# Two-layer encoder trunk on one core: where exponentials, reciprocals, a norm's operands, key copies and the first parameters are issued

## The chip, the core and the metric

One NeuronCore of a Trainium2 chip. The metric is the device time of one execution in microseconds (us). The engines of the core run side by side, each taking its own queue of instructions in order: TensorE (PE in the profile, with its weight loads as PEld), VectorE (DVE), ScalarE (ACT), GpSimd (POOL) and SyncE (SP), which here issues DMA transfers. They meet at semaphores.

## The reference, cut to what matters

The input is 512 tokens of width 1024, with 256 memory tokens. Each of two layers adds three terms to `x`:

```python
for l in range(DEPTH):
    x = x + hybrid_mixer(rms_norm(x, norm_mix[l]), w_in[l], na_rpb[l], q_norm[l], k_norm[l], w_out[l], ...)
    x = x + memory_cross_attention(rms_norm(x, norm_mem_q[l]), rms_norm(mem, norm_mem_kv[l]), w_q, w_kv, w_o)
    x = x + conv_ffn(rms_norm(x, norm_ffn[l]), w_up[l], conv_w[l], conv_b[l], w_down[l])
return rms_norm(x, norm_final)
```

The mixer projects `h` once to six parts. Eight heads do a 2-D neighbourhood attention (NA) with a learned bias, `softmax(q k / 8 + bias) v` over a window of the 8 x 64 grid. Eight query heads over two key heads do full attention (GQA); there q and k are normalised per head and rotated (rope) first. Both results go through `w_out`. The memory attention has 4 heads over 256 tokens; the feed-forward part is a SwiGLU with a depthwise convolution of width 3. Everything is float32.

## The kernel before

**Precision.** A float32 product is made of three matmuls. Each operand is split into `hi` (rounded to the type fp32r) and `lo = value - hi`, and `mm3` (L374) issues hi·hi, hi·lo and lo·hi into one PSUM bank. Weights are split by `emit_split`: `hi` by ACT (L290), `lo` mostly by POOL (L291).

**Layout.** `x` lies transposed in eight tiles `xT[c]` of 128 features x 512 tokens. A projection is 8 features' chunks x 3 matmuls = 24 matmuls of 128x512. PSUM has eight banks: four with tag `mm`, two `sc` (scores), two `tr` (transposes and small sums).

**Order.** PE's instructions keep the order in which the program writes them (`Counted`), as do those of engines named `..._IN_ORDER`. The instructions of ACT, DVE and POOL are put in order by a list scheduler that simulates the engines and picks by priority; `behind(n)` gives the instructions in its block a priority n places later (earlier for a negative n), and `tc.issue_after(i)` forces those of the same engine behind instruction `i`. Buffers from a pool (`tmp()`: 14 slots of 128x512; `ps_mm()`: 4 banks) are taken when the scheduler comes to the first instruction that writes them.

**Start (L386 to L405, L613 to L638).** `FIRST` lists the loads of the first three weights, cut in pieces, and of the eight `xT`. All are issued by SP, but the first weight piece and, behind it, the eight gains of the first norm, `par[:, 0, 0:8]` (L404), by ACT. `Norm.operand` (L464) makes `hi = x·gain` on ACT and `lo = x·gain - hi` on DVE.

**NA stage.** `weave` (L170) runs the four units' steps: in step s, `na_transpose(s-2)`, a piece of filler, `na_normalise(s-1)`, `na_scores(s)`, filler, `na_values(s-2)`, filler. A filler piece is some 2.5 us of matmuls from the projections (`project_qk`, `project_v`, `gqa_project`). `na_scores` (L778) writes two `sc` banks, DVE adds the bias and takes minima (L797), ACT takes four exponentials with their sums (L803). `na_normalise` (L807) takes the reciprocal of the sums on DVE (L809) and scales on POOL (L522) and ACT (L815). `na_values` (L834) multiplies by v into `mm` banks; ACT copies half of each (L849), DVE adds (L850, L851).

**Projections.** `split_qk` evicts q and k: ACT writes hi (`split_q` L738, `split_k` L720 and L722), DVE lo (L740, L724, L726). K is wanted in both halves of the partitions. For the very first k (`near`) ACT and DVE write both halves; for all others SP doubles it by DMA. `project_v` evicts with L518 (ACT) and L519 (DVE). `gqa_rope` (L895) reads its bank three times: two DVE products L901 and L902, then ACT's squares L903; a later piece, `split` (L933), multiplies the rotated value by its norm (L934). `reads` collects ACT's readings of PSUM banks in program order.

**Memory norm.** `memory_prepare` (L555) makes hi and lo of the 8 chunks of the memory (128x256 each): hi on ACT (L567), lo on DVE (L568), two chunks a step while the NA stage ends.

Of the kernel before, what the change touches and what calls it, by code (L numbers as in the profile page):

```python
# [18 lines left out]
P = 128  # L19
# [164 lines left out]
def encoder_kernel(ctx: ExitStack, tc: tile.TileContext, t: dict, out: bass.AP):  # L184
# [198 lines left out]
            mm3(ps, wh[:, k, c], wl[:, k, c], *ops[k], k == first, k == last)  # L383


    xT = [xpool.tile([P, S], F32, tag=f"x{c}", name=f"xT{c}") for c in range(KC)]  # L386
    par = cpool.tile([P, DEPTH, NPAR], F32, name="par")
    ones = cpool.tile([P, 1], F32, name="ones")
    nc.vector.memset(ones, 1.0)
# [3 lines left out]
    first_loads = []  # L393
    for n in FIRST:
        if isinstance(n, int):
            SP.dma_start(xT[n], t["xT"][n * P : (n + 1) * P, :])
            continue
        u, k0, k1 = n
        if u == len(first_loads):
            first_loads.append(raw_tile())  # L400
        raw, loads = first_loads[u]
        (nc.scalar if n == FIRST[1] else SP).dma_start(raw[:, k0:k1], loads[0][1][:, k0:k1])
        if n == FIRST[1]:
            nc.scalar.dma_start(par[:, 0, 0:8], t["par"][:, 0, 0:8])  # L404
    ACT_IN_ORDER.copy(small(1), ones)  # L405
    qkg = cpool.tile([P, DEPTH, 2], F32, name="qkg")
    gfin = cpool.tile([P, KC], F32, name="gfin")
# [37 lines left out]
    class Norm:  # L445


        def __init__(self, gcol=None, l=None, cols=slice(0, S)):
            self.gcol, self.l, self.acc, self.last, self.cols, self.n = gcol, l, None, None, cols, cols.stop - cols.start
            if gcol is not None:  # L450
                self.hi, self.lo = [xpool.tile([P, KC, S], F32R, tag="xg", name=nm("xg"), bufs=2) for _ in range(2)]
                self.ops = [(self.hi[:, c, :], self.lo[:, c, :]) for c in range(KC)]

        def close(self, c, pm):


            DVE.tensor_add(pm, pm, xT[c])
            DVE.tensor_copy(xT[c], pm)
            closed.append(self.operand(c, src=pm, rank=-25).ins)
            self.square(c)  # L460
            if c == KC - 1:
                closed.clear()

        def operand(self, c, act=ACT, src=None, dve=DVE, hi_only=False, lo_only=False, rank=0):  # L464
            src = xT[c] if src is None else src
            g = par[:, self.l, self.gcol + c : self.gcol + c + 1]
            hi, lo = self.ops[c]
            e = None if lo_only else act.activation(hi, src, AF.Copy, scale=g)
            if not hi_only:
                with behind(rank):  # L470
                    dve.scalar_tensor_tensor(lo, src, g, f(hi), op0=ALU.mult, op1=ALU.subtract)
            return e
# [82 lines left out]
    def memory_prepare(l):  # L555

        mops.clear()
        raw = load_mem()
        yield
        for c in range(KC):  # L560
            if c % 2 == 0:
                mg = rtile((2, 2, MEMN))
            g = par[:, l, G_MKV + c : G_MKV + c + 1]
            hi, lo = mg[:, 0, c % 2, :], mg[:, 1, c % 2, :]
            src = raw[c // 4][:, c % 4, :]
            with behind(40):
                ACT.activation(hi, src, AF.Copy, scale=g)  # L567
                DVE.scalar_tensor_tensor(lo, src, g, f(hi), op0=ALU.mult, op1=ALU.subtract)  # L568
            mops.append((hi, lo))
            if c % 2 == 1:  # L570
                yield

    mem_rstd = cpool.tile([P, MB], F32, name="mem_rstd")
# [38 lines left out]

    warm_up(N_WARM)  # L613
    nn = Norm(G_MIX, 0)
    DVE_IN_ORDER = InOrder(tc, nc.vector)
    for n in FIRST:
        if isinstance(n, int):
# [25 lines left out]
    for l in range(DEPTH):  # L643
# [73 lines left out]
        def split_k(pm, kt, near):  # L717
            rows = [(slice(64 * j, 64 * j + 64), slice(64 - 64 * j, 128 - 64 * j)) for j in range(2)]
            for k, (r, o) in zip(kt, rows):
                read(ACT.copy(k[r, 0], pm[r]))  # L720
                if near:
                    ACT.copy(k[o, 0], pm[r])  # L722
            for k, (r, o) in zip(kt, rows):
                DVE.tensor_sub(k[r, 1], pm[r], f(k[r, 0]))  # L724
                if near:
                    DVE.tensor_sub(k[o, 1], pm[r], f(k[r, 0]))  # L726

            def double():
                for k, (r, o) in zip(kt, rows):
                    SP.dma_start(f(k[o]), f(k[r]))  # L730

            if not near:
                late(2, double)
# [44 lines left out]
        def na_scores(u):  # L778
            p, bp = divmod(u, 2)
            if bp == 0 and p + 1 < 4:  # L780
                load_bias(p + 1)
            qst, kst = qk["q", p], qk["k", p]
            sc = [ps_s().rearrange("p (i n) -> p i n", i=2) for _ in range(2)]
            for i in range(2):
                b = 2 * bp + i
                qs, ks = slice(b * P, b * P + P), slice(WIN[b], WIN[b] + 256)
                for j in range(2):
                    for part in range(2):
                        PE.matmul(sc[j][:, i, :], qst[j][:, qs], kst[2 * part + j][:, ks], start=part == 0, stop=part == 1)
            nmx, sums = small(4), small(4)  # L790
            es = [tmp((2, 256)) for _ in range(2)]
            with behind(30):
                for j in range(2):
                    for i in range(2):
                        b = 2 * bp + i
                        col = slice(2 * j + i, 2 * j + i + 1)
                        DVE.tensor_tensor_reduce(  # L797
                            out=sc[j][:, i, :], in0=sc[j][:, i, :], in1=bias[p][j][:, WTYPE[b], :],
                            op0=ALU.add, op1=ALU.min, scale=-1.0, scalar=BIG, accum_out=nmx[:, col])
                for j in range(2):  # L800
                    for i in range(2):
                        col = slice(2 * j + i, 2 * j + i + 1)
                        ACT.activation(es[j][:, i, :], sc[j][:, i, :], AF.Exp, bias=nmx[:, col], scale=-1.0,  # L803
                                       accum_out=sums[:, col])
            na[u] = es, sums

        def na_normalise(u):  # L807
            es, sums = na[u]
            DVE.reciprocal(sums, sums)  # L809
            for j in range(2):  # L810
                for i in range(2):
                    if i or j:
                        normalise(es[j][:, i, :], sums, 2 * j + i, POOL)
                    else:
                        ACT.activation(es[j][:, i, :], es[j][:, i, :], AF.Copy, scale=sums[:, 2 * j + i : 2 * j + i + 1])  # L815
            na[u] = es
# [43 lines left out]

        gq, gk, gvt, gtab = [None] * 4, [], [], []

        def gqa_eps():


# [29 lines left out]
        def gqa_rope(g, pm):  # L895
# [3 lines left out]
            xs, sq, cc = tmp(), tmp(), tmp()  # L899
            with behind(-20):  # L900
                DVE.scalar_tensor_tensor(xs, pm, gain, gtab[0][:, 1], op0=ALU.mult, op1=ALU.mult)  # L901
                DVE.scalar_tensor_tensor(cc, pm, gain, gtab[0][:, 0], op0=ALU.mult, op1=ALU.mult)  # L902
                read(ACT.activation(sq, pm, AF.Square))  # L903

            def swap():
# [58 lines left out]

        def gqa_normalise(u):
            es, sums = ga[u]
            DVE.reciprocal(sums, sums)
            for j in range(2):
                normalise(es[j], sums, j, POOL)
            ga[u] = es  # L970
# [147 lines left out]
            return [NA_FILL] * 3  # L1118

        woven[0] = True  # L1120
        weave(8, [(2, na_transpose), None, (1, na_normalise), (0, na_scores), None, (2, na_values), None], attn_fill.run, na_quanta)
        weave(4 * NB, [(2, gqa_transpose_p), (1, gqa_normalise), (0, gqa_scores), (3, lambda u: gqa_values(u, 0)),
                       (4, lambda u: gqa_values(u, 1)), None], attn_fill.pace, lambda s: [GQA_SLOT[s]])
        woven[0] = False
# [332 lines left out]
```

## Time and profile before

| what | value |
|---|---|
| device time, median of 3 runs | 1366.57 us (1366.39 to 1367.67) |
| the profiled execution: its own time | 1367.86 us |
| its span, first to last instruction | 1366.1 us |
| DVE, ACT, POOL busy | 877.3, 675.0, 688.1 us (64%, 49%, 50% of the span) |
| bytes moved, mean rate | 139.88 MB, 102 GB/s |
| busy of 20 us from 100 to 120 us: PE, DVE, ACT, POOL | 18.59, 14.38, 11.84, 14.78 us |
| busy of 343 us from 342 to 685 us (first layer's feed-forward and the start of the second layer): PE | 343.00 us |

A row of the timeline reads: start in us, duration in us, engine, line, operation, what it writes `<-` what it reads, shape, count, and in brackets how long the engine had been idle before it and what released it. `PEclk` is the clock that TensorE was granted, 1.00 being full speed. The first layer's NA stage runs from about 40 to 150 us, its GQA stage to 246 us; the second layer's NA stage from about 712 to 815 us. Matmuls are pipelined: a row's duration is longer than the distance to the next row, and the distance is what counts.

### The profile page before, as it was taken

What the parts mean: (1) busy time and instruction counts of PE and PEld (TensorE: products, weight loads), DVE (VectorE), ACT (ScalarE), POOL (GpSimd) and SP (SyncE); (2) the same over time, 40 slices, a digit from 0 to 9 for tenths busy, and PEclk for the clock granted to TensorE, in tenths of its full rate; (3) what the DMA queues carried; (4) which work ended last, traced back from release to release, by engine and by line L of the source; (5) the groups of instructions that cost most, each with busy time, mean ns of one, the idle gap of its engine ahead of it and who ended that gap; (6) DMA issues with size and microseconds to landing.
All of it is one profiled execution on the core that took longest, in us unless ns stands there. A gap on an engine that the chain in (4) does not pass through costs nothing.

```text
span 1366.1 us, 19239 instructions
## 1 busy us (share of the span) xinstructions
PE 1349.0 (99%) x7082; PEld 1157.5 (85%) x7082; DVE 877.3 (64%) x1542; ACT 675.0 (49%) x1258; POOL 688.1 (50%) x491
## 2 busy tenths in 40 slices
PE   9999999999999999999999999999999999999998
PEld 7888899888888888888888988998888888888897
DVE  6665776665886188357546777746758834861874
ACT  6675577564543144234456667756644423432441
POOL 2466657636444444444554676657264444444441
PEclk9999999999999999999999999999999999999999
DMA  6753213322333333333347532133143333323331
GB/s 215 212 169 99 77 47 86 86 77 77 104 98 93 95 98 92 102 94 98 87 121 227 140 101 70 57 100 94 31 123 93 101 100 93 101 84 109 93 92 63
DMA packets 219358, 139.88 MB, mean 102 GB/s; under 512 B 6144, under 2 KB 212224, under 8 KB 219264
## 3 DMA queue, kind: packets, MB, share of 16 engines
q1 hardware_dynamic: 218432, 138.13, 34.5%
q8 instruction: 56, 0.92, 0.3%
q10 hardware_dynamic: 832, 0.53, 0.1%
q14 instruction: 38, 0.31, 0.1%
HBM read 126.05 MB, written 2.10 MB: 94 GB/s over the span
## 4 chain that ended last, share of the span: by engine, by line
PE 91%; DVE 3%; ACT 3%; DMA 2%; issue 1%; SPq 0%; POOL 0%; DVEq 0%; ACTq 0%
PE mm L77 80%; PE sc L77 6%; PE tr L64 3%; PE tr L77 1%; DMA raw<-in_w_in 1%; DMA t<-in_memT 1%; ACT t L803 1%; ACT hi L290 0%; SPq L64 0%; DMA xT<-in_xT 0%; DVE t L487 0%; ACT r L515 0%; DVE sc L797 0%; DVE r L740 0%; ACT r L738 0%
## 5 line engine op out<-in xcount | busy, mean ns | idle before, releaser
L291 POOL TENSOR_TENSOR lo<-raw,hi 128x1024 fp32r<-128x1024 f32 (+2 forms) x268 | 499.9, 1876 | 477.1 <-ACT hi L290 472.7
L77 PE MATMUL mm<-xg,hi 128*128 128x512 f32 x1920 | 596.6, 392 | 0.0
L77 PEld LDWEIGHTS mm<-xg,hi 128*128 128x128 f32 x1920 | 356.7, 188 | 70.8
L290 ACT CAST hi<-raw 128x512 fp32r<-128x512 f32 (+2 forms) x276 | 224.1, 836 | 309.5 <-PE mm L77 256.3
L77 PE MATMUL mm<-xg,lo 128*128 128x512 f32 x960 | 374.5, 390 | 0.0
L77 PE MATMUL mm<-r,hi 128*128 128x512 f32 (+1 forms) x1096 | 316.6, 373 | 0.0
L77 PEld LDWEIGHTS mm<-r,hi 128*128 128x128 f32 x1096 | 198.3, 189 | 34.7 <-DVE r L516 0.4
L1281 DVE SCALAR_TENSOR_TENSOR t<-t,par,t 128x7 f32<-128x7 f32 (+1 forms) x352 | 201.8, 641 | 34.0 <-ACT t L1274 34.0
L77 PEld LDWEIGHTS mm<-xg,lo 128*128 128x128 f32 x960 | 180.7, 188 | 38.2
L77 PE MATMUL mm<-r,lo 128*128 128x512 f32 (+1 forms) x548 | 203.5, 371 | 0.0
L77 PEld LDWEIGHTS mm<-r,lo 128*128 128x128 f32 x548 | 103.3, 188 | 17.8
L1266 DVE TENSOR_TENSOR t<-mm,rep 128x512 f32<-128x512 f32 x88 | 60.1, 687 | 78.6 <-PE mm L77 62.3
L522 POOL TENSOR_SCALAR t<-t,s 128x512 f32<-128x512 f32 (+1 forms) x112 | 66.8, 610 | 78.0 <-DVE s L809 36.8
L1287 DVE TENSOR_TENSOR r<-t,r 128x512 fp32r<-128x512 f32 x44 | 90.2, 2049 | 7.3 <-ACT r L1286 4.1
L1283 ACT ACTIVATE t<-t 128x512 f32<-128x512 f32 x44 | 27.9, 633 | 134.4 <-DVE t L1281 134.3
L1310 DVE TENSOR_TENSOR xT<-xT,mm 128x512 f32<-128x512 f32 x32 | 21.9, 685 | 106.8 <-PE mm L77 106.8
L77 PE MATMUL sc<-r,r 128*128 128x256 f32 (+1 forms) x352 | 70.0, 332 | 0.0
L1274 ACT ACTIVATE t<-t,par 128x512 f32<-128x512 f32 x88 | 66.8, 806 | 3.3 <-DVE t L1266 3.3
L64 PE MATMUL tr<-ident,t 128*128 128x128 f32 x456 | 62.0, 276 | 2.3 <-DVE t L522 0.9
L77 PE MATMUL mm<-r,r 128*128 128x256 f32 (+1 forms) x428 | 61.9, 297 | 2.4 <-ACT t L903 2.4
L64 PEld LDWEIGHTS tr<-ident,t 128*128 128x128 f32 x456 | 53.3, 142 | 10.5 <-issue 2.9
L77 PEld LDWEIGHTS mm<-r,r 128*128 128x128 f32 x428 | 56.3, 191 | 5.1 <-ACT t L903 2.6
(156 smaller groups left out, 1618.2 us busy)
## 6 DMA issues: line engine op xcount, KB each, us to landing
raw<-in_w_up SPq DMA_DIRECT2D x88, 512.0 KB, 3.7
raw<-in_w_in SPq DMA_DIRECT2D x33, 512.0 KB, 3.9
raw<-in_w_down SPq DMA_DIRECT2D x32, 448.0 KB, 3.6
raw<-in_w_mem_kv SPq DMA_DIRECT2D x16, 512.0 KB, 3.6
raw<-in_w_down SPq DMA_DIRECT2D x16, 512.0 KB, 3.9
r<-in_bias SPq DMA_DIRECT2D x16, 384.0 KB, 5.6
r<-r SPq DMA_DIRECT2D x22, 256.0 KB, 5.0
raw<-in_w_out SPq DMA_DIRECT2D x8, 512.0 KB, 3.6
```

Source lines behind the costliest of these rows:

```text
L64: return lambda *a, **k: self.tc.keep_in_program_order(op(*a, **k))
L77: return self.tc.keep_in_program_order(self.engine.matmul(out, lhsT, rhs, **k))
L290: act.copy(hi[:, k], raw[:, k])
L291: (POOL if eng[0] == "P" else DVE).tensor_sub(lo[:, k], raw[:, k], f(hi)[:, k])
L522: eng.tensor_scalar(e, e, sums[:, col : col + 1], 1.0, op0=ALU.mult, op1=ALU.mult)
L803: ACT.activation(es[j][:, i, :], sc[j][:, i, :], AF.Exp, bias=nmx[:, col], scale=-1.0, accum_out=sums[:, col])
L1266: DVE.tensor_mul(u, us[side], ffn.rep)
L1274: ACT.activation(cc, u, AF.Identity, bias=par[:, l, CB + ch : CB + ch + 1], scale=w[1])
L1281: DVE.scalar_tensor_tensor(cc[:, dst], u[:, src], wi, cc[:, dst], op0=ALU.mult, op1=ALU.add)
L1283: ACT.activation(cs[0], cs[0], AF.Silu)
L1287: DVE.tensor_sub(acts[j][1], cs[0], f(acts[j][0]))
L1310: DVE.tensor_add(xT[m], xT[m], pm)
```

## The change

Six edits, in one diff.

- The gains of the first norm travel as eight more columns of the first x tile (`x0`, rows of 520 floats); ACT's second DMA is gone, and `nn.gain` of the first norm reads them there.
- `memory_prepare` scales a chunk in place on ACT, and after each second chunk copies both to hi with one ACT instruction of 128x512 and makes lo with one POOL subtraction of 128x512. DVE has no part in it.
- For the first k, the second half's lo is copied by POOL from the first half's instead of being computed a second time by DVE.
- The four NA exponentials leave `na_scores`; they become a step of their own, `na_exponentials`, written behind the second piece of filler, and are forced behind the last reading of a PSUM bank that ACT has been given so far. Their output tiles are asked for there, too.
- The reciprocals of NA and of GQA are forced behind the last L902 written so far (`turned`).

```diff
-    xT = [xpool.tile([P, S], F32, tag=f"x{c}", name=f"xT{c}") for c in range(KC)]
+    x0 = xpool.tile([P, S + KC], F32, tag="x0", name="xT0")
+    xT = [x0[:, :S]] + [xpool.tile([P, S], F32, tag=f"x{c}", name=f"xT{c}") for c in range(1, KC)]
...
-            SP.dma_start(xT[n], t["xT"][n * P : (n + 1) * P, :])
+            if n == 0:
+                SP.dma_start(x0, t["x0"])
+            else:
+                SP.dma_start(xT[n], t["xT"][n * P : (n + 1) * P, :])
...
-        if n == FIRST[1]:
-            nc.scalar.dma_start(par[:, 0, 0:8], t["par"][:, 0, 0:8])
...
+        def gain(self, c):
+            return par[:, self.l, self.gcol + c : self.gcol + c + 1]
...
-            g = par[:, self.l, self.gcol + c : self.gcol + c + 1]
+            g = self.gain(c)
...
-            g = par[:, l, G_MKV + c : G_MKV + c + 1]
-            hi, lo = mg[:, 0, c % 2, :], mg[:, 1, c % 2, :]
             src = raw[c // 4][:, c % 4, :]
             with behind(40):
-                ACT.activation(hi, src, AF.Copy, scale=g)
-                DVE.scalar_tensor_tensor(lo, src, g, f(hi), op0=ALU.mult, op1=ALU.subtract)
-            mops.append((hi, lo))
+                ACT.activation(src, src, AF.Copy, scale=par[:, l, G_MKV + c : G_MKV + c + 1])
             if c % 2 == 1:
+                src = raw[c // 4][:, c % 4 - 1 : c % 4 + 1, :]
+                with behind(40):
+                    ACT.copy(mg[:, 0], src)
+                    POOL.tensor_sub(mg[:, 1], src, f(mg[:, 0]))
+                mops.extend((mg[:, 0, i, :], mg[:, 1, i, :]) for i in range(2))
                 yield
...
+    nn.gain = lambda c: x0[:, S + c : S + c + 1]
...
                 if near:
-                    DVE.tensor_sub(k[o, 1], pm[r], f(k[r, 0]))
+                    with behind(-40):
+                        POOL.tensor_copy(k[o, 1], k[r, 1])
...
-            nmx, sums = small(4), small(4)
-            es = [tmp((2, 256)) for _ in range(2)]
+            nmx = small(4)
...
+            na[u] = sc, nmx
+
+        def na_exponentials(u):
+
+            sc, nmx = na[u]
+            sums = small(4)
+            es = [tmp((2, 256)) for _ in range(2)]
+            with behind(30), tc.issue_after(reads[-1]) if reads else nullcontext():
                 for j in range(2):
                     for i in range(2):
...
         def na_normalise(u):
             es, sums = na[u]
-            DVE.reciprocal(sums, sums)
+            with tc.issue_after(turned[-1]) if turned else nullcontext():
+                DVE.reciprocal(sums, sums)
...
+        turned = []
...
-                DVE.scalar_tensor_tensor(cc, pm, gain, gtab[0][:, 0], op0=ALU.mult, op1=ALU.mult)
+                turned.append(DVE.scalar_tensor_tensor(cc, pm, gain, gtab[0][:, 0], op0=ALU.mult, op1=ALU.mult).ins)
...
         def gqa_normalise(u):
             es, sums = ga[u]
-            DVE.reciprocal(sums, sums)
+            with tc.issue_after(turned[-1]):
+                DVE.reciprocal(sums, sums)
...
-        weave(8, [(2, na_transpose), None, (1, na_normalise), (0, na_scores), None, (2, na_values), None], attn_fill.run, na_quanta)
+        weave(8, [(2, na_transpose), None, (1, na_normalise), (0, na_scores), None, (0, na_exponentials), (2, na_values),
+                  None], attn_fill.run, na_quanta)
...
+    arrays["x0"] = np.concatenate([arrays["xT"][:P], arrays["par"][:, 0, :KC]], axis=1)
```

## The prediction

> **What bounds the kernel now.** I read the page's busy times first, then PE's waits, then the granted clock, then the timeline around each wait.
>
> ```profile
> span 1366.1 us, 19239 instructions
> PE   1349.0 (99%) x7082; PEld 1157.5 (85%) x7082; DVE 877.3 (64%) x1542; ACT 675.0 (49%) x1258; POOL 688.1 (50%) x491
> ```
>
> PE is the bound everywhere, and the change takes no matmul away. What can be won is therefore PE's idle time, 1366.1 - 1349.0 = 17.1 us, part of which is the empty head and tail, and time in which PE runs below full rate. The waits of PE, from the view that sums them by releaser over the whole span:
>
> ```profile
> PE mm L77 <- ACT t L903: 2.4, 1, 2.4
> PE mm L77 <- DVE r L740: 1.4, 1, 1.4
> PE mm L77 <- ACT r L518: 1.3, 1, 1.3
> PE sc L77 <- ACT xg L64: 1.0, 1, 1.0
> PE tr L64 <- DVE xg L516: 0.7, 1, 0.7
> PE tr L77 <- ACT t L903: 0.8, 1, 0.8
> ```
>
> The columns are total, times, longest. Each is one event, so each can be looked up. Then the clock, in three stretches (PE busy is the second number, the granted clock stands behind the five engines):
>
> ```profile
> 33.00:41.00 8.00, 6.59 (x55) 6.39 (x55) 7.08 (x11) 5.66 (x11) 2.54 (x3) 1.00 0.33 96
> 119.00:122.40 3.40, 1.43 (x8) 1.30 (x9) 2.06 (x4) 2.03 (x5) 2.88 (x5) 1.00 0.23 58
> 122.40:129.30 6.90, 6.90 (x26) 6.07 (x26) 2.22 (x5) 2.06 (x5) 5.51 (x5) 0.51 0.52 161
> ```
>
> Right behind the longest wait PE runs 6.9 us at 0.51: 6.9 x 0.49 = 3.4 us of work lost. The 1.4 us wait inside the first stretch left the clock at 1.00. So the 2.4 us wait seems to cost 5.8 us.
>
> **The change, part by part.**
>
> *First parameters.*
>
> ```profile
> xT<-in_xT SPq DMA_DIRECT2D x1, 256.0 KB, 2.9
> par<-in_par ACTq DMA_DIRECT2D x1, 4.0 KB, 3.6
> ...
> 0.72 0.88 SPq L64 DMA_DIRECT2D xT<-in_xT  x2
> 1.21 0.49 ACTq L404 DMA_DIRECT2D par<-in_par  x1
> 4.93 1.34 ACT L64 ACTIVATE xg<-xT,par 128x512 fp32r<-128x512 f32 x2 [1.72 <-DMA par<-in_par]
> 5.70 0.80 PE L77 MATMUL sc<-xg,hi 128*128 128x512 f32 x1 [1.00 <-ACT xg L64]
> 6.72 1.91 PE L77 MATMUL sc<-xg,hi 128*128 128x512 f32 x4
> 6.17 0.39 ACT L64 CAST hi<-raw 128x256 fp32r<-128x256 f32 x1
> ```
>
> The gains land at 1.21 + 3.6 = 4.8 us, the first x tile at 0.72 + 2.9 = 3.6. With the gains inside that tile (1.6% more bytes) ACT starts at about 3.7 and PE's first product at 4.5 in place of 5.70: 1.2 us. Lower down: the second weight's hi is ready at 6.17 + 0.39 = 6.56 whatever the gains do, and PE, at this stage at half rate (the four matmuls from 6.72 stand (1.91 - 0.63) / 3 = 0.43 us apart, 0.63 being one's duration), needs it at its fifth matmul, the third being at 6.72: now at 7.58. So 1.0 us survives there, and 0.5 if the clock rises when it does now, since matmuls brought forward then run at half rate. I take 0.8, bounds 0.5 and 1.2. SP's queue keeps its issues; ACT's loses one.
>
> *K's copies.*
>
> ```profile
> 35.13 0.68 DVE L726 TENSOR_TENSOR r<-sc,r 64x512 fp32r<-64x512 f32 x1
> ...
> 36.53 0.69 DVE L726 TENSOR_TENSOR r<-sc,r 64x512 fp32r<-64x512 f32 x1
> 37.26 1.39 DVE L740 TENSOR_TENSOR r<-mm,r 64x512 fp32r<-64x512 f32 x2
> ...
> 36.31 2.51 POOL L291 TENSOR_TENSOR lo<-raw,hi 128x512 fp32r<-128x512 f32 x2 [3.29 <-ACT hi L290]
> ...
> L920 POOL COPY t<-s x10: 602/610/618, 106.5 to 828.5; 128x512 f32<-128x512 f32 x10
> ```
>
> DVE works from 35.13 to 38.65 without a break, and PE waits 1.4 us for the last of it, a bank that L740 reads. The two L726 go: 0.68 + 0.69 = 1.4 us earlier, all of the wait. The two POOL copies fall into POOL's 3.29 us of idle time. A POOL copy of 64x512 is not in the trace; it lies between 0.3 us (half of L920's 0.61 us for 128x512) and the 1.26 us of one subtraction at 36.31. I take 0.6, L920 being the nearer row. At worst 2.5 us begin at 35.1 and push a weight split by 1.3 us, and k's lo is read only by the scores three us later. Gain 1.4, bounds 0.7 and 1.4.
>
> *Exponentials.*
>
> ```profile
> 85.68 0.48 ACT L803 ACTIVATE t<-sc,s 128x256 f32<-128x256 f32 x1
> 86.27 0.76 ACT L849 COPY t<-mm 64x256 f32<-64x256 f32 x2
> ...
> 86.67 0.87 DVE L850 TENSOR_TENSOR t<-mm,t 64x256 f32<-64x256 f32 x2 [0.21 <-ACT t L849]
> 87.57 0.87 DVE L851 TENSOR_TENSOR t<-mm,t 64x256 f32<-64x256 f32 x2
> ...
> 785.39 0.47 ACT L803 ACTIVATE t<-sc,s 128x256 f32<-128x256 f32 x1 [3.28 <-DVE s L797]
> 787.21 0.61 ACT L903 ACTIVATE t<-mm 128x512 f32<-128x512 f32 x1
> ```
>
> At 86.6 PE wants an `mm` bank; its chain is four exponentials on ACT, L849 behind them, L850 twice, L851, end 88.0. The view names L518; that comes at nearly the same moment. Written later than now, the exponentials no longer outrank L849, which could start two us sooner: the wait of 1.3 us goes. But only readings written *before* them are forced ahead, and L849 is written after; bounds 0 and 1.3, I take 1.3, as the lower rank is written out. At 785 L903 stands behind the exponentials and PE waits 0.8 us for it; here the order is forced: 0.8, bounds 0.3 and 0.8. Behind the moved exponentials wait the reciprocal, POOL's scaling and the transposes; those are a whole step (some 10 us) later. The new order can also make ACT stand: where the reading that the exponentials are forced behind is an L903, it waits for L902, and the exponentials and whatever the scheduler put behind them (L849, L518) with it, and for those PE waits at its `mm` banks.
>
> *Reciprocals.*
>
> ```profile
> 117.94 0.18 DVE L809 RECIPROCAL s<-s 128x4 f32<-128x4 f32 x1 [1.60 <-ACT t L803]
> 118.22 0.70 DVE L934 TENSOR_TENSOR mm<-t,mm 128x512 f32<-128x512 f32 x1
> 118.82 0.75 DVE L901 SCALAR_TENSOR_TENSOR t<-mm,qkg,r 128x512 f32<-128x512 f32 x1
> 119.48 0.74 DVE L902 SCALAR_TENSOR_TENSOR t<-mm,qkg,r 128x512 f32<-128x512 f32 x1
> ...
> 116.84 0.39 PE L77 MATMUL mm<-xg,lo 128*128 128x512 f32 x1
> 117.88 0.71 PE L77 MATMUL mm<-r,r 128*128 128x256 f32 x4
> 120.97 0.74 PE L77 MATMUL mm<-r,r 128*128 128x256 f32 x4 [2.38 <-ACT t L903]
> ```
>
> This is the 2.4 us wait. The bank that L901 and L902 read is complete at 116.84 + 0.39 = 117.23, but DVE sits 1.60 us at the reciprocal, which waits for the exponentials. With both out of the way L901 starts at 117.25, L902 (0.66 from start to start) ends at 118.65, L903 (0.61) at 119.35, and PE goes on at 119.4, not 120.97: 1.6 us, and a wait of 0.8 us, shorter than the one that kept the clock at 1.00, so the 3.4 us as well: 5.0. The other bound: L934, whose bank PE fills until 117.9, stays ahead of L901; then only about 0.3 us is won. L901 follows L934 without a wait of its own, as if its output took a `tmp` slot that L934 frees, and two slots fewer are held by the exponentials now. I take 5.0, bounds 0.3 and 5.8.
>
> *Memory operands.* Per layer eight DVE products go, four ACT copies of 128x512 (0.61 us, as L903 of that shape) and four POOL subtractions (1.26) come.
>
> ```profile
> L568 DVE SCALAR_TENSOR_TENSOR r<-r,par,r x16: 477/668/1523, 95.8 to 798.1; 128x256 fp32r<-128x256 f32 x16
> ```
>
> (Least, median, most ns.) DVE loses 8 x 0.67 = 5.3 us a layer, POOL gains 4 x 1.26 = 5.0 and ACT 4 x 0.61 = 2.4. All lie beside PE's work: cover is POOL's half-empty time, and weights split there are read over 10 us later. I cost it at nothing (-0.5 to 0.5), its share in the two L903 waits being counted above. [...]
>
> **Sum.** 0.8 + 1.4 + 1.3 + 0.8 + 5.0 = 9.3 us. The profiled execution took 1367.86 us (span 1366.1 and 1.8 around it), so 1358.6. The median of the runs is 1.3 us below that execution; I keep the 1.3 us for small new waits of the reordered queues. Lower bounds give 0.5 + 0.7 + 0 + 0.3 + 0.3 - 0.5 = 1.3, upper ones 1.2 + 1.4 + 1.3 + 0.8 + 5.8 + 0.5 = 11.0.
>
> **Rivals.**
> 1. *L934 stays first.* The rope wait and the slow clock stay: 9.3 - 5.0 + 0.3 = 4.6 us, 1363.3. For it: the order of today, which no edit touches directly. Against: the missing wait of L901.
> 2. *The slow clock does not come from the wait.* Then 3.4 us stay: 1362.0. Against it: it begins within 1.5 us of the wait's end. [...]
> 3. *Given back at the start of GQA.* At 163 us PE already waits 0.7 us for L516, in a DVE backlog that the change leaves; if all that the first layer won is lost there, 0.8 us remain: 1367.1. Against: that backlog starts from PE's own scores and moves with them.
> 4. *The order is the same as today.* The scheduler finds the exponentials the same places: start and k alone, 1365.7.
> 5. *Slower: the score banks come free too late.*
>
> ```profile
> 79.17 1.12 PE L77 MATMUL sc<-r,r 128*128 128x256 f32 x8
> 91.08 1.12 PE L77 MATMUL sc<-r,r 128*128 128x256 f32 x8
> ```
>
> The banks written at 79.17 are free when the exponentials end, at 86.2; they are wanted at 91.08. A delay over 4.8 us makes PE wait at every one of the 14 following scores of both layers. At the rope above the exponentials would end 3.4 us later than now. At 0.7 us over, 14 x 0.7 = 9.8 us, less 2.2 for start and k: 1375.5.
>
> **How the numbers follow.** Forecast 0.42; rivals 0.22, 0.08, 0.08, 0.06, 0.14 in this order. About 0.2% (2.7 us) is what a measurement tells from no change. Faster, below 1363.8: 0.42 + 0.22 + 0.08 = 0.72, less some for small losses, 0.70. Within: 0.16. Slower: 0.14. The likeliest case's own range is 1355 to 1361. The range goes from 1354 (all upper bounds from the median, 1366.57 - 11.0 = 1355.6, and a little for the clock at the start) to 1366, which leaves out rival 5 and the end of rival 3.
>
> **What would show it.** The first product at 4.5 us; no L726 and no wait on L740 near 37; L849 ahead of L803 near 85; L901 and L902 ahead of L809 and L934 near 117, a wait under 1 us there and the clock at 1.00 from 112 to 135; no wait on L903 in the second layer. The prediction is wrong if PE waits for L803 at its scores, or for POOL at a transpose or weight, or if the clock falls elsewhere.

## The result, and the profile after

The changed kernel takes 1374.74 us (median of 6 runs, 1371.48 to 1377.80), the kernel before beside it 1366.48 us (6 runs, 1364.84 to 1368.02): a ratio of 1.0060, 95% interval 1.0041 to 1.0079. It is slower by 8.3 us, above the whole range. A second series (`r1_changed` below) gave 1.0056 (1.0041 to 1.0071). The profiled execution took 1377.23 us. Its page:

```profile
span 1375.4 us, 19250 instructions
PE 1350.0 (98%) x7082; PEld 1156.4 (84%) x7082; DVE 863.4 (63%) x1524; ACT 678.2 (49%) x1266; POOL 698.5 (51%) x501
```

PE's busy time has hardly changed (1349.0 before); its idle time grew from 17.1 to 25.4 us. The longest of PE's waits (total, times, longest, in us) show where:

```profile
PE mm L77 <- ACT hi L290: 2.7, 1, 2.7
PE mm L77 <- ACT t L922: 2.4, 1, 2.4
PE mm L77 <- DVE r L522: 1.6, 1, 1.6
...
PE tr L77 <- DVE t L493: 1.5, 1, 1.5
PE mm L77 <- ACT r L524: 1.5, 1, 1.5
PE mm L77 <- DVE r L749: 1.4, 1, 1.4
PE mm L77 <- DVE r L525: 1.4, 1, 1.4
...
PE mm L77 <- DVE t L868: 1.0, 1, 1.0
```

L922, L524 and L749 are the lines L903, L518 and L740 of before, whose waits the prediction took away: all three are still there. The others shown are new. PE runs the same 7082 matmuls in the same order in both kernels, so the start of each can be subtracted from the start of the same one before. This difference is called the lag here:

| at (us, before) | step of the lag | lag of the changed kernel behind it |
|---|---|---|
| 5.7, first product | -1.18 | -1.18 (-1.88 by 10 us) |
| 24.1, squares' sum | +1.64 | -0.18 |
| 62.5, a projection behind L522 | +1.79 | 1.73 |
| 77.7, a projection behind L868 | +1.12 | 2.95 |
| 99.8, a product behind L290 | +2.82 | 6.32 |
| 140 to 760 (6.8 us at a granted clock of 0.50 lie before 140 in either trace and cancel) | | 6.3 to 6.84 |
| 766.7, second layer, a product behind L525 | +1.59 | 8.44 |
| 779.0, transposes | +0.68 | 9.35 |
| 787.9, no wait for L903 | -0.95 | 8.40 |

The largest step is at 99.8. The timeline of the changed kernel there:

```profile
98.25 1.71 ACT L571 ACTIVATE r<-r,par 128x256 f32<-128x256 f32 x4 [3.00 <-DMA r<-in_memT]
...
100.67 1.71 ACT L571 ACTIVATE r<-r,par 128x256 f32<-128x256 f32 x4 [0.71 <-DMA r<-in_memT]
...
102.29 0.45 ACT L819 ACTIVATE t<-sc,s 128x256 f32<-128x256 f32 x1
...
104.08 0.62 ACT L575 CAST r<-r 128x512 fp32r<-128x512 f32 x1
...
104.78 1.27 POOL L576 TENSOR_TENSOR r<-r,r 128x512 fp32r<-128x512 f32 x1 [8.19 <-ACT r L575]
105.00 1.14 ACT L290 CAST hi<-raw 128x512 fp32r<-128x512 f32 x2
...
106.14 1.19 PE L77 MATMUL mm<-xg,hi 128*128 128x512 f32 x2 [2.66 <-ACT hi L290]
```

All eight scalings of the layer stand together, in two groups of four, and each group waits for its half of the memory to land; the exponentials, the copy L575 and the weight split L290 stand in the same queue behind them. POOL stands 8.19 us for L575, and PE waits for the split. In the second layer it is the same with another end: ACT stands 4.25 us at the scalings, L524 comes behind them at 774.11, DVE's L525 waits for it, and PE for L525. In the kernel before they went in pairs, with other work between:

```profile
95.28 0.92 ACT L567 ACTIVATE r<-r,par 128x256 fp32r<-128x256 f32 x2
...
100.37 0.92 ACT L567 ACTIVATE r<-r,par 128x256 fp32r<-128x256 f32 x2
```

What the changed line waited for, over both layers (least, median, most ns; first and last start):

```profile
L571 ACT ACTIVATE r<-r,par x16: 492/494/511, 98.2 to 773.7; 128x256 f32<-128x256 f32 x16
its engine sat idle before it (us, times) until:
  DMA r<-in_memT: 8.0, 4
```

L567 waited for no transfer (no idle time for one ahead of any of its 16). Ahead of the smaller new losses, at 62.5 and 77.7, ACT also stands for a transfer, of the memory for its norm; the rows of the first:

```profile
54.35 0.63 ACT L590 ACTIVATE t<-t 128x512 f32<-128x512 f32 x1 [5.47 <-DMA t<-in_memT]
...
56.06 0.47 ACT L819 ACTIVATE t<-sc,s 128x256 f32<-128x256 f32 x1
...
63.47 0.68 DVE L522 TENSOR_TENSOR r<-tr,r 128x512 fp32r<-128x512 f32 x1
...
64.21 0.51 PE L77 MATMUL mm<-r,r 128*128 128x256 f32 x2 [1.64 <-DVE r L522]
```

In the kernel before, ACT stood there 3.61 us:

```profile
51.20 0.63 ACT L583 ACTIVATE t<-t 128x512 f32<-128x512 f32 x1 [3.61 <-DMA t<-in_memT]
```

The square is now 3.15 us later, and the exponentials start at 56.06 behind it. The last place is that of the predicted 5.0 us, the rope:

```profile
126.11 0.69 DVE L953 TENSOR_TENSOR mm<-t,mm 128x512 f32<-128x512 f32 x1 [2.65 <-POOL t L943]
126.71 0.74 DVE L920 SCALAR_TENSOR_TENSOR t<-mm,qkg,r 128x512 f32<-128x512 f32 x1
...
128.21 0.60 ACT L922 ACTIVATE t<-mm 128x512 f32<-128x512 f32 x1 [6.65 <-DVE t L921]
...
128.86 0.74 PE L77 MATMUL mm<-r,r 128*128 128x256 f32 x4 [2.37 <-ACT t L922]
```

The reciprocal is out of the way, but L953 (L934 of before) still stands ahead of the two products, and now it is POOL that it waits for. That is rival 1.

### The profile page after: what moved, and what is told of

It reads as the page before. It is cut to its first block, busy times and chain, and to the rows that moved or that the text cites. A ratio compares the mean times of both kernels' runs of the same rounds, so it can differ in the third digit from the quotient of the medians.

```text
span 1375.4 us, 19250 instructions
## 1 busy us (share of the span) xinstructions
PE 1350.0 (98%) x7082; PEld 1156.4 (84%) x7082; DVE 863.4 (63%) x1524; ACT 678.2 (49%) x1266; POOL 698.5 (51%) x501
## 4 chain that ended last, share of the span: by engine, by line
PE 86%; DMA 4%; DVE 3%; ACT 3%; issue 1%; POOL 1%; SPq 0%; DVEq 0%; ACTq 0%; POOLq 0%
PE mm L77 76%; PE sc L77 6%; PE tr L64 3%; DMA t<-in_memT 1%; DMA r<-in_memT 1%; PE tr L77 1%; DMA xT<-in_xT 1%; ACT t L819 1%; ACT hi L290 1%; SPq L64 0%; DMA raw<-in_w_in 0%; DVE r L732 0%; DVE t L493 0%; DMA raw<-in_w_down 0%; DVE lo L291 0%
## 5 line engine op out<-in xcount | busy, mean ns | idle before, releaser
L290 ACT CAST hi<-raw 128x512 fp32r<-128x512 f32 (+2 forms) x276 | 223.9, 836 | 314.6 <-PE mm L77 245.9
```

Of the source, the lines that this page charges most:

```text
L290: act.copy(hi[:, k], raw[:, k])
```

## Experiments

The edits are numbered by the five points of the list under The change: 1 the gains, 2 the memory operands, 3 k's copies, 4 the exponentials, 5 the reciprocals. The theories, as the expectations name them. T1: the in-place scalings need no output slot, so nothing spaces them in ACT's queue, and they block it. T2: the exponentials' later place costs by itself. T3: the start's other order of loads costs. T4: ACT standing at the norm's squares costs. R1: the memory edit costs by its own work. R2: the memory's transfers land later. All kernels compute the whole reference. Each ratio is against the kernel before on the same chip; 0.001 is 1.37 us.

### The parts alone

`m1_mem_only`: edit 2 alone.

```diff
-                ACT.activation(hi, src, AF.Copy, scale=g)
-                DVE.scalar_tensor_tensor(lo, src, g, f(hi), op0=ALU.mult, op1=ALU.subtract)
+                ACT.activation(src, src, AF.Copy, scale=par[:, l, G_MKV + c : G_MKV + c + 1])
...
+                    ACT.copy(mg[:, 0], src)
+                    POOL.tensor_sub(mg[:, 1], src, f(mg[:, 0]))
```

> The kernel before with the memory operands' edit alone (scaling in place on ACT, hi by one ACT copy, lo by one POOL subtraction per two chunks); nothing is left out of the computation. T1, the scalings: an in-place scaling takes no output slot, so nothing holds it back in the scheduler's order; all eight stand together near 98 us in ACT's queue, ACT stands there until the memory's DMAs have landed, and weight splits and exponentials behind them come late. Then this kernel is slower than the one before by 4 to 8 us, PE waits over 1.5 us near 104 us for a hi of L290 or a result behind it, and the scalings' row shows an idle time of 4 us or more put down to the DMA of the memory. T2, the exponentials' place: no loss here, within 1 us of the kernel before. T3, the start: no loss here, within 1 us.

1369.18 against 1365.87 us, 1.0024 (1.0014 to 1.0034): 3.3 us slower, less than expected, by the expected way. ACT stands at the scalings, and PE waits 2.4 us for the L290 behind them. The timeline:

```profile
97.56 1.71 ACT L565 ACTIVATE r<-r,par 128x256 f32<-128x256 f32 x4 [4.70 <-DMA r<-in_memT]
```

`m2_no_mem`: the changed kernel with these lines as they were before (the reverse of that diff).

> The changed kernel with the memory operands as they were (hi on ACT, lo on DVE, into fresh slots); nothing is left out of the computation. T1, the scalings: the loss goes with them, the time is 1 us above to 3 us below the kernel before, and PE's wait for a hi of L290 near 104 us is gone. T2, the exponentials' place: the loss stays, 5 to 9 us above the kernel before, with PE waits near 62 and 78 us. T3, the start: the loss stays, too, 5 us or more.

1368.40 us, 1.0016 (1.0007 to 1.0025). The wait for L290 is gone, but 2.2 us of loss stay where T1 allowed 1: between T1 and T2, and the losses near 62 and 78 us (1.54 and 0.75 in the lag) are there.

`m3_exp_only`: edits 4 and 5 alone.

```diff
+        def na_exponentials(u):
...
+            with behind(30), tc.issue_after(reads[-1]) if reads else nullcontext():
...
+            with tc.issue_after(turned[-1]) if turned else nullcontext():
+                DVE.reciprocal(sums, sums)
```

> The kernel before with the exponentials' and the reciprocals' edits alone; nothing is left out of the computation. T1, the scalings: within 1.5 us of the kernel before on either side: the wait on L903 near 786 us is gone (0.8 us), but the product L934 keeps its place ahead of L901, so the wait of about 2.4 us near 118 us and the half clock behind it stay. T2, the exponentials' place: slower by 4 us or more, PE waiting near 62 and 78 us for DVE, whose inputs stand behind a forced exponential on ACT. T3: within 1 us.

1365.23 us, 0.9997 (0.9986 to 1.0008). T2 falls as the cause of the whole: by themselves the two edits cost and win nothing that the times show. It is a balance: in the profile's lag they win 1.0 us near 88 us and 0.95 near 788, and lose 1.0 near 62 and 0.7 near 779. The wait near 786 us is gone, the one near 118 us is not (2.4 us, on L913), as expected.

`m4_start_k`: edits 1 and 3 alone.

```diff
+    x0 = xpool.tile([P, S + KC], F32, tag="x0", name="xT0")
...
-                    DVE.tensor_sub(k[o, 1], pm[r], f(k[r, 0]))
+                    with behind(-40):
+                        POOL.tensor_copy(k[o, 1], k[r, 1])
```

> The kernel before with the gains inside the first x tile and k's copies on POOL alone; nothing is left out of the computation. T1, the scalings: the first product is at 4.5 us, but the 1.2 us are given back at the sum of the squares near 22 us, which waits for the last x tile, and the wait near 37 us stays since ACT waits there for a weight's landing: within 1 us of the kernel before. T2: the same. T3, the start: the loads issued earlier change the order of the landings, and PE waits near 62 and 78 us for results behind a reading of memory that has not landed: slower by 3 us or more.

1366.43 us, 1.0005 (0.9995 to 1.0016). T3 falls, too. The first product was 1.12 us earlier, the squares' sum took 1.40 back:

```profile
23.44 1.05 PE L77 MATMUL tr<-ones,t 128*128 128x1 f32 x8 [1.25 <-DVE t L492]
```

Alone, the three parts cost 3.3, -0.6 and 0.6 us, together 3.3; the whole costs 8.

### Repairs inside the changed kernel

`r1_changed`, the changed kernel again, beside the next three.

> The changed kernel as it is, on the same chip as its neighbours, with which it is compared; nothing is left out. All theories: 1372 to 1378 us, 6 to 11 us above the kernel before.

1374.41 against 1366.52 us, 1.0056 (1.0041 to 1.0071).

`m5_mem_paced`:

```diff
-            with behind(40):
+            with behind(40), tc.issue_after(reads[-1]):
                 ACT.activation(src, src, AF.Copy, scale=par[:, l, G_MKV + c : G_MKV + c + 1])
```

> The changed kernel with each in-place scaling of the memory forced behind the last reading of a PSUM bank written so far, so that the eight are spread over ACT's queue again; nothing is left out. T1, the bunching: the wait for a hi of L290 near 104 us falls under 0.5 us, that near 773 us goes, and the time is 3 to 6 us below the changed kernel of this call. Rival R1, the work itself (four ACT copies and four POOL subtractions a layer more, DVE's products fewer): the loss stays, within 1.5 us of the changed kernel, with PE waiting for POOL or ACT at the same places. Rival R2, the memory's transfers land later than before: the wait stays, wherever the scalings stand.

1370.98 us, 1.0032 (1.0020 to 1.0045), 3.4 us below the changed kernel: T1, within its bounds. ACT no longer stands at the scalings, and both waits behind them, PE's for L290 near 106 us and for DVE's lo of v (L525) near 774, are gone. The memory's transfers are issued at 87.5 us, later than before (85.3), and no scaling waits for them: R2 falls. But where the force put two of them (the second at 112.31), L520's copies come late, and with them DVE's L521 and PE:

```profile
111.51 0.50 ACT L570 ACTIVATE r<-r,par 128x256 f32<-128x256 f32 x1
...
112.84 0.62 ACT L574 CAST r<-r 128x512 fp32r<-128x512 f32 x1
113.36 1.07 ACT L520 CAST r<-tr 128x512 fp32r<-128x512 f32 x2
...
116.85 1.04 PE L77 MATMUL tr<-pairs,t 128*128 128x2 f32 x8 [2.20 <-DVE r L521]
```

`m9_stat_early`:

```diff
-            sq = tmp((2, MEMN))
-            SP.dma_start(sq, t["memT"][i * 256 : (i + 1) * 256, :]...)
+            while len(sqs) < min(i + 2, KC // 2):
+                n = len(sqs)
+                sqs.append(tmp((2, MEMN)))
+                SP.dma_start(sqs[n], t["memT"][n * 256 : (n + 1) * 256, :]...)
+            sq = sqs[i]
             yield
```

> The changed kernel with each load of the memory norm's squares issued one step of the NA stage (some 12 us) earlier; nothing is left out. T4, that ACT stands at the squares (5.5 us near 54 us) until a load of 8 us has landed, with the exponentials behind it: the PE waits near 62 us (1.8 us) and 78 us (1.1 us) go, and the time is 2 to 3.5 us below the changed kernel of this call, the wait near 104 us staying. Rival T2, the exponentials' later place delays the scores by itself: the waits stay and the time is within 1 us of the changed kernel's.

1374.75 us, 1.0056 (1.0040 to 1.0072): no gain, a miss of the number. In its trace PE is ahead at 99 us, by 3.4 us of the changed kernel's first profile and by 1.5 of its second; but 1.7 and 0.2 us of that stand at 61 us already, so 1.7 and 1.3 are won near 62 and 78, less than T4's 2 to 3.5. The scalings wait for a transfer that does not come sooner than in the second of these profiles (the first scaling starts at 96.6 us; there at 96.2, in the first at 98.2), and PE's wait for the split is 4.7 us, where it was 2.7 and 3.6.

`m14_paced_early`: both diffs together.

> The changed kernel with both repairs: the in-place scalings spread over ACT's queue, and the loads of the memory norm's squares one step earlier; nothing is left out. T4 with T1 (what the earlier loads won near 62 and 78 us was lost again near 104 us only because ACT stood there for the scalings): the waits near 62 and 104 us are both gone and the time is 2 to 3 us below that of the paced kernel alone, 1368 to 1369 us. Rival, that the two losses are independent of the memory's loads: as the paced kernel alone, 1370 to 1372 us.

1370.12 against 1366.08 us, 1.0027 (1.0016 to 1.0038), not to be told from the paced kernel's 1.0032. So T4's 2 to 3 us are not confirmed as a gain even where the scalings are out of the way: this kernel has other waits, 1.74 us on L752 near 38 us and 0.63 on L521 near 73, and it keeps the paced kernel's wait of 2.2 us for L521's lo near 118.

### The rope's order

`m13_exp_rope`: `m3_exp_only` and one line more.

```diff
             def split(xr, pr):
-                DVE.tensor_mul(pr, xr, pr)
+                with tc.issue_after(turned[-1]):
+                    DVE.tensor_mul(pr, xr, pr)
```

> The kernel before with the exponentials' and the reciprocals' edits, and the rope's last product L934 forced behind the L902 written last; nothing is left out. The prediction's step on the reciprocals (L901 and L902 could start at once when the bank is complete): the wait near 118 us falls from 2.4 to 0.8 us or less, the clock stays at 1.00 there, and the time is 2 to 5 us below the kernel before. Rival: DVE's two products start no earlier, since their tiles or the bank come late, or L934 behind them becomes the wait: within 1 us of the kernel before.

1363.99 against 1366.52 us, 0.9985 (0.9977 to 0.9994). With the order that the prediction assumed, the wait is what it said (0.8) or less, 0.21 us:

```profile
116.59 0.75 DVE L911 SCALAR_TENSOR_TENSOR t<-mm,qkg,r 128x512 f32<-128x512 f32 x1 [0.40 <-PE mm L77]
...
118.10 0.70 DVE L945 TENSOR_TENSOR mm<-t,mm 128x512 f32<-128x512 f32 x1
...
118.75 0.74 PE L77 MATMUL mm<-r,r 128*128 128x256 f32 x4 [0.21 <-ACT t L913]
```

`m7_rope_first`: that line alone in the kernel before (with the list `turned`).

> The kernel before with one edit that the change does not make: L934 forced behind the L902 written last; nothing is left out. If the order of L934 alone makes the wait near 118 us: 2 to 4 us below the kernel before, as with the exponentials' edit. Rival, that the reciprocal ahead (1.6 us of waiting for the exponentials) takes its place without the other edits: the wait stays over 1.5 us, and the time within 1 us of the kernel before.

1364.14 against 1366.08 us, 0.9987 (0.9978 to 0.9996). The time, 1.9 us below, is just short of what the first theory has, the wait is as the rival has it: the reciprocal, ahead of the products, now holds the squares up (L905, L903 of before), and 1.57 us are left. Both must go for the wait to go.

```profile
119.55 0.18 DVE L809 RECIPROCAL s<-s 128x4 f32<-128x4 f32 x1 [1.60 <-ACT t L803]
...
121.77 0.51 PE L77 MATMUL mm<-r,r 128*128 128x256 f32 x2 [1.57 <-ACT t L905]
```

Two combinations: `m12_nomem_early_rope` (the changed kernel, the memory operands as before, with the two diffs of `m9` and `m13`) and `m10_all_repairs` (the changed kernel with all three).

> The changed kernel without the memory operands' edit, with the loads of the squares one step earlier and L934 behind L902; nothing is left out. T1 and T4 leave no loss then, and the rope's order wins: 1361 to 1364 us, with no wait of PE over 1.5 us behind 40 us. Rival, the start's and k's edits cost in the NA stage by something other than these loads: 1365 to 1368 us.

> The changed kernel with all three repairs (scalings spread, squares' loads one step earlier, L934 behind L902); nothing is left out. T1, T4 and the rope's order add up: 1364 to 1367 us. Rival, the memory edit's own work still costs where ACT and DVE are late: 1368 us or more.

1366.81 us, 1.0000 (0.9991 to 1.0009), and 1369.38 us, 1.0026 (1.0016 to 1.0035). Both went to the rival. Two questions stayed: why the memory edit costs 2.6 us even when spread, and why edits 1 and 3 cost beside the exponentials.

### A slot for the scalings

`m18_mem_slot`: `m1_mem_only`, but each pair of scalings writes into a slot of the pool that L567 wrote to. ACT's and POOL's work is unchanged.

```diff
+                sl = rtile((2, 2, MEMN), F32)[:, 0]
...
-                ACT.activation(src, src, AF.Copy, scale=par[:, l, G_MKV + c : G_MKV + c + 1])
+                ACT.activation(sl[:, c % 2, :], raw[c // 4][:, c % 4, :], AF.Copy, scale=par[:, l, G_MKV + c : G_MKV + c + 1])
             if c % 2 == 1:
+                src = sl
```

> The kernel before with the memory edit, except that each pair of scalings writes into a slot of its own (pool r, as L567's did) and not in place; ACT's and POOL's work is that of the edit, nothing is left out. T1, the missing slot: ACT's idle time at the scalings falls from 8 to 10 us to under 2.5 us, the wait for a hi of L290 near 104 us is gone, and the time is 2 to 4 us below the memory edit alone (which stood 3.3 us above the kernel before), within 1.5 us of the kernel before. Rival R1, the work: the time stays 2.5 us or more above the kernel before, PE waiting for ACT or POOL behind the scalings.

1364.01 against 1366.87 us, 0.9981 (0.9971 to 0.9990): faster than before, and 0.0043, 5.9 us, below the same edit in place (1.0024). The scalings are pairs again, and wait 0.2 us where they waited 7.3 in place (timeline, then what the line waited for):

```profile
96.00 0.91 ACT L564 ACTIVATE r<-r,par 128x256 f32<-128x256 f32 x2 [0.17 <-DMA r<-in_memT]
...
101.54 0.93 ACT L564 ACTIVATE r<-r,par 128x256 f32<-128x256 f32 x2
```
```profile
its engine sat idle before it (us, times) until:
  DMA r<-in_memT: 0.2, 1
```

`m20_changed_slot`: the same in the changed kernel.

> The changed kernel with a slot for each pair of scalings in the same way; nothing is left out. T1: 1368 to 1370 us, 4 to 6 us below the changed kernel, the waits near 104 and 773 us gone. Rival R1: 1371 us or more, as with the forced spreading or above it.

1367.97 us, 1.0007 (0.9997 to 1.0016): 0.0049, 6.7 us, of the changed kernel's loss are gone. T1 stands and R1 falls: the work is the same, only the slot differs. The forced spreading of `m5` had a price of its own place.

These runs also show what T4 is. The changed kernel, `r1`, `m5` and `m20` run the same instructions in the same order on ACT, DVE and POOL until the scalings begin. Up to 93 us their profiles are four executions of one program (all in us):

| profile | ACT stands at the memory norm's squares, first and second time | PE waits near 62 and 78 | ACT goes on with a weight's split at | PE waits near 38 |
|---|---|---|---|---|
| changed kernel | 5.47, 4.01 | 1.6, 1.0 | 31.12 | 1.4 |
| `r1` | 4.17, 4.90 | 0.4, 1.8 | 29.60 | 0.4 |
| `m5` | 3.65, 4.04 | 0, 1.0 | 29.71 | 0 |
| `m20` | 3.45, 3.39 | 0, 0.2 | 29.55 | 0 |

The longer ACT stands for the transfer, the longer PE waits: T4's link is there, but it cost between 0.2 and 2.6 us, by the execution. The profile of `m20` is that of its fastest run, so its small waits are in part luck; the 6.7 us are a difference of medians.

### What is left

`m15_exp_rope_start` and `m16_exp_rope_k`: `m13_exp_rope` with edit 1, or with edit 3.

> The kernel before with the exponentials' and the reciprocals' edits, the rope's order and the gains inside the first x tile; nothing is left out. If the start's edit is what costs beside the exponentials (its loads land otherwise): 1366 us or more, with the waits near 65 to 88 us. If k's copies are: 1363 to 1365 us.

> The kernel before with the exponentials' and the reciprocals' edits, the rope's order and k's copies on POOL; nothing is left out. If k's copies are what costs beside the exponentials: 1366 us or more. If the start's edit is: 1362 to 1364 us, and this is the fastest of all.

1365.36 us, 0.9991 (0.9981 to 1.0001), between the two theories' times, and 1363.19 us, 0.9974 (0.9963 to 0.9985), as the second theory has it, against 1366.87. K's copies are not what costs, the start's edit may be: 2.2 us lie between the two. Beside `m13` (0.9985) k's copies win 1.5 us and the start's edit loses 0.8, but these intervals overlap. The profiles do not show k's gain: against `m13` it is 0.6 us near 38 us, but PE waits 1.5 us near 88 us where `m13` and `m15` wait 0.3, and 0.45 us longer near 127. Near 88 us PE waits 1.2 to 1.5 us in every kernel that has edits 3 and 4 together, so there the gain of the one is undone beside the other; why is open. The profile of `m15` shows one way in which the start's edit costs: the wait at the squares (1.3 us) is followed by 3.4 us at a granted clock of 0.50. The columns are PE, PEld, DVE, ACT and POOL busy, granted clock, DMA share and GB/s.

```profile
22.68:26.09 3.41, 2.41 (x15) 2.14 (x16) 2.52 (x6) 0.00 (x0) 1.43 (x2) 1.00 0.52 160
26.09:29.51 3.42, 3.42 (x12) 2.85 (x11) 0.00 (x0) 1.14 (x2) 2.08 (x2) 0.50 0.90 274
```

From 26 to 36 us the mean clock is 0.83 in `m15`; it is 1.00 in `m4` and in the changed kernel, which have this edit too, and in before, `m16` and `m22`, which do not. In this one profile it costs 1.7 us; what it costs in the mean is not shown, and the rest stays open.

`m21_parts_that_won` has all edits but the start's, and with them the slot and the rope's order; `m22_without_exponentials` is the same without edits 4 and 5.

> All edits but the start's, the scalings with a slot for each pair, and L934 behind L902; nothing is left out. If the gains add up: memory edit with a slot 2.9, exponentials, rope and k 3.7 us, so 6 us below the kernel before, 1359 to 1362 us. Rival, that all of them win the same idle time in the NA stage: 3 to 4 us below, 1363 to 1364 us.

> The same without the exponentials' and the reciprocals' edits; nothing is left out. If the exponentials' edit has a share (the wait near 786 us, 0.8 us, and less waiting near 62 us): 0.5 to 2 us above the kernel beside it. Rival, that it has none: within 0.5 us of it.

1362.59 us, 0.9978 (0.9969 to 0.9987), and 1361.04 us, 0.9968 (0.9955 to 0.9980), against 1365.90. The gains do not add up to 6 us; the 3.3 us are what the rival has. For `m22` both theories miss: it is not slower by the edit's share or equal, but 1.5 us faster, though the intervals overlap. In the trace of `m21` PE waits where the changed kernel does, near 62 us. In that of `m22` it does not, although ACT stands 5.99 us at the squares there, longer than in any row of the table above. So that wait needs the exponentials' edit, too.

```profile
62.11 0.74 PE L77 MATMUL mm<-r,r 128*128 128x256 f32 x4 [1.19 <-DVE r L516]
```

`m22`, with five runs, is the fastest version found, 4.9 us below the kernel before.

## Why the prediction was wrong, by its own steps

Between 9.3 us won and 8.3 us lost lie 17.6 us. Roughly, since medians and single profiles are mixed here, 6.7 of them are the memory operands, 5.0 the rope, 1.3 the exponentials near 88 us, 1.4 k's copies and 0.6 the start; in the profile 2.9 more are lost near 62 and 78 us, for which the prediction had no term.

**Memory operands, costed at nothing: the step that failed.** "All lie beside PE's work" counted what the instructions take and not where they would stand. The cover (weights split there are read over 10 us later) was measured on a queue in which the scalings were spaced. What spaced them was the output slot that the scheduler had to find for each pair, and the edit removes it. The price is 6.7 us (`m20` against the changed kernel). The lag gives the same from inside: 2.82 us at 99.8, half of the 3.41 us at a granted clock of 0.50 behind it (1.7), 1.59 in the second layer, 6.1 in all. The work itself, which the prediction weighed, costs nothing visible (`m18`). `m18` has all of POOL's new subtractions and is 2.9 us faster than before.

**Reciprocals, 5.0 us.** Rival 1 happened: L934 stayed ahead of L901. The argument against it, that L901 waits for the tmp slot that L934 frees, was not the reason for the order; forcing the order is what moved it (`m13`). The wait itself was sized well, 2.17 us won in place of 1.6. The 3.4 us of clock were not a fixed price: see the last section.

**Exponentials at 86, 1.3 us.** L819 still stands ahead of L866 there, the wait on L524 is 1.5 us: the lower bound, 0. The step "as the lower rank is written out" chose the wrong end. In `m3`, `m13` and `m15` the wait falls to 0.3 us with L849 still behind the exponentials, so the size was near, but the path was another and was lost beside k's copies. That they would come later near 56 us, behind a square that waits for the memory, was not foreseen.

**Layer 2, 0.8 us.** Right: 0.95 won at 787.9. `m18` has that gain without the exponentials' edit and `m3` without the memory's, so either is enough for it.

**Start, 0.8 us.** The first product is at 4.52 as predicted, 1.88 us are won by 10 us, and all but 0.2 of it is lost by 23.9. The working stopped at PE's fifth matmul and did not ask what is late next: the squares' sum.

```profile
19.60 3.31 DVE L487 TENSOR_TENSOR t<-t,t 128x512 f32<-128x512 f32 x2
```
```profile
19.76 4.08 DVE L493 TENSOR_TENSOR t<-t,t 128x512 f32<-128x512 f32 x3
```

The first row is of before, the second of after. Before, the sum is ready at 22.91 and PE comes at 24.07; now PE comes 1.8 us earlier and the sum at 23.84.

**K's copies, 1.4 us.** L726 is gone from DVE. In the first profile of the changed kernel the chain ahead of it is later by as much, since ACT stands for a weight until 31.12, so PE still waits 1.4 us for L749. That is this execution: in the three others of the table PE waits 0.4, 0 and 0 us. Over the twenty profiles the wait near 38 us is 1.35 us in the mean without edit 3 and 0.6 with it. So the mechanism was right, and the gain at this place is some 0.75 us, near the lower bound.

```profile
31.12 1.14 ACT L290 CAST hi<-raw 128x512 fp32r<-128x512 f32 x2 [2.70 <-DMA raw<-in_w_in]
```

**Rival 5** had the sign and nearly the time (1375.5), but by luck: PE did not wait at its scores for banks.

## What to carry to other kernels

An in-place rewrite also takes away the buffer that paced the instruction in an in-order queue (6.7 us here). When an edit removes a slot, ask what then comes first in that queue, and which transfer it waits for. An earlier start is worth only as much as the next thing that is late (of 1.88 us won by 10 us, 0.18 were left at 24); and parts that win alone need not add up (3.3 us together, not 6). ACT's first stand for a transfer at the memory norm's squares took 5.47, 4.17, 3.65 and 3.45 us in four profiles of the same instructions, so a second profile is worth its while before such a wait is explained.

## What the hardware showed that was not expected

The same wait did not always come with the same clock. In the profile of before the granted clock is 0.50 from 122.44 to 129.26 us and again from 1361.48; in that of after it is 0.50 from 105.89 to 109.30, from 129.78 to 133.19, and again from 1372.23. The two in the profile of after last 3.41 us each and begin 23.89 us apart, seven times that; the first in that of before lasts twice 3.41. Stretches of 3.41 us in three kernels, before, `m4_start_k` and after, all three with the same wait of 2.4 us at the rope:

```profile
119.02:122.44 3.42, 1.47 (x8) 1.33 (x9) 2.04 (x4) 2.07 (x5) 2.90 (x5) 1.00 0.23 58
122.44:125.85 3.41, 3.41 (x13) 2.88 (x11) 0.84 (x2) 0.31 (x1) 3.22 (x3) 0.50 0.62 187
```
```profile
114.86:118.27 3.41, 2.39 (x17) 2.02 (x15) 1.72 (x7) 2.22 (x9) 3.04 (x5) 1.00 0.00 0
118.27:121.69 3.42, 2.06 (x11) 1.82 (x12) 1.70 (x4) 2.38 (x5) 2.90 (x3) 1.00 0.32 77
121.69:125.10 3.41, 3.41 (x25) 3.05 (x24) 1.50 (x5) 1.37 (x3) 3.41 (x4) 1.00 0.71 217
```
```profile
126.37:129.78 3.41, 1.04 (x7) 0.88 (x7) 1.75 (x3) 1.57 (x6) 1.14 (x2) 1.00 0.16 38
129.78:133.19 3.41, 3.41 (x11) 2.66 (x10) 1.45 (x5) 3.23 (x9) 1.73 (x4) 0.50 0.62 161
```

In before and after, where one of these stretches has 1.95 and 2.37 us of PE's idle time, the next has a granted clock of 0.50; in `m4`, where two have 1.02 and 1.36 us, the clock stays at 1.00. Of the kernels with this wait of 2.4 us, before, after and `m3` have a mean clock of 0.84, 0.92 and 0.92 from 119 to 140 us, `m1`, `m2` and `m4` 1.00. So in these profiles a wait of this size came with 0 (`m4`), 1.7 (after, half of 3.41) or 3.4 us (before, half of 6.82) beside itself, and the prediction's rival 2 was right in that the wait alone does not decide. That the place of the wait among the stretches makes the difference is an estimate from the rows above. The idle time alone does not decide, either: 1.00 us was followed by 0.50 near 25 us in the `m15` rows above, while 1.48 us from 20.55 to 23.96 in the changed kernel was followed by 1.00, and 1.41 us from 33 to 41 in before left the clock at 1.00; why is open.
